# Expert loop of a mixture-of-experts block: the next round's gather and the last round's spread issued in parts between the up products

## The chip, the cores and the metric

The kernel runs on one core of a Trainium2 chip. Its engines are TensorE (PE), VectorE (DVE), ScalarE (ACT), GpSimd (POOL) and SyncE (SP), which here issues the loads. The metric is the device time of one execution in microseconds, the median of several runs; the time before is 2066.87 us.

## The reference

Two transformer blocks on 512 tokens of width 1024 in float32. The first has two kinds of attention and then a mixture of experts, which is where the change is:

```python
g_w, g_idx = lax.top_k(g_prob, 1)
top_v, top_i = lax.top_k(e_sel, TOP_K)
gate = (g_w * jax.nn.softmax(top_v, axis=-1)).reshape(-1)
def expert_block(args):
    xb, e = args
    return (jax.nn.silu(xb @ w1[e]) * (xb @ w3[e])) @ w2[e]
out = jnp.zeros((T + 1, D), jnp.float32).at[row_token].add(row_gate[:, None] * ys.astype(jnp.float32))
```

There are 64 experts; w1 and w3 are 1024 x 512 each and w2 is 512 x 1024, so one expert's weights are 6 MB and all of them 384 MB. The second block (retention and latent attention, a feed-forward layer and a gated projection) follows.

## The kernel before

The expert loop (`for q in range(NQ)`) handles four experts in each of 16 rounds, with room for 32 tokens of each, so that the four fill 128 rows or columns.

- **Loads.** A round has 24 loads of 1,024 KB: 8 pieces of w1, 8 of w3, 8 of w2 (two halves `hf` for each of four experts). `moe_load_to(n)` issues them on SyncE in that order (lines 866 and 880; 871 in the last round), into the pool `L` of 16 buffers. It is called before each half of a product with a look-ahead of `AHEAD` = 13 loads; `moe_lim` caps it until the path for overfull experts is behind. A load waits until the buffer that it takes has been read for the last time, and for the load eight before it, since SyncE counts its loads on eight semaphores in turn.
- **Up products.** `moe_up(q, k, n0)` (line 1029) multiplies the gathered tokens `xT` with w1 (k = 1) or w3 (k = 3), in two halves of 4 loads; a function handed in as `between` runs between the halves. The w1 result `p1` and the w3 result `p3` give `hd` (lines 1263 to 1265), which is transposed into `hT` (lines 1270 and 1272).
- **Gather.** `moe_gather(q)` (line 1016) picks the tokens of a round's experts by products with the 0/1 tables `oh` of `places_oh(q)` (line 998), in two halves of 32 instructions.
- **Back product.** `moe_back(q)` (line 1043) multiplies `hT` with w2 into `y`.
- **Spread.** `moe_spread(q)` transposes the gate tables `ohg` (line 1065, copied by ScalarE to `gt`), multiplies them with `y` (line 1072) and adds the result to the tokens `acc` on VectorE (line 1077), for four blocks of tokens and two halves of the width.

TensorE takes its instructions in the order of the code. In round q that is: up product 1, up product 3, both halves of the gather for round q + 1, the transposes of `hd`, the gate transposes and the whole spread of round q - 1, the back product. Every load buffer of w1 and w3 comes free at the end of a half product, those of w2 in the back product.

**The path for overfull experts.** After round 8 (`REST_AT`), `moe_rest()` loads the largest number of tokens of any expert (line 1089) into a register of each engine and, only if it is over 32, runs a body that handles what is left over (`tc.If`, line 1090). With these inputs the body isn't run. Its buffers come from the same pools as the loop's.

## Time and profile before

| what | value |
|---|---|
| median of 3 runs | 2066.87 us (2065.31 to 2069.51) |
| the profiled execution | 2066.38 us, span 2064.6 us |
| granted TensorE clock, mean of the span | 0.969 |
| TensorE busy | 1896.4 us (92% of the span) |
| VectorE, ScalarE busy | 746.8 us (36%), 468.8 us (23%) |
| moved by DMA | 510.16 MB, 247 GB/s over the span |

The profile is of one execution. A busy share is an average over stages with different limits, so the expert loop, roughly from 410 to 1365 us, is read by itself: which wait ends last there, and when SyncE may issue. Granted clock 1.00 stands for 2.4 GHz and 0.50 for 1.2 GHz.

### The profile page before, as it was taken

What the parts mean: (1) busy time and instruction counts of PE and PEld (TensorE: products, weight loads), DVE (VectorE), ACT (ScalarE), POOL (GpSimd) and SP (SyncE); (2) the same over time, 40 slices, a digit from 0 to 9 for tenths busy, and PEclk for the clock granted to TensorE, in tenths of its full rate; (3) what the DMA queues carried; (4) which work ended last, traced back from release to release, by engine and by line L of the source; (5) the groups of instructions that cost most, each with busy time, mean ns of one, the idle gap of its engine ahead of it and who ended that gap; (6) DMA issues with size and microseconds to landing.
All of it is one profiled execution on the core that took longest, in us unless ns stands there. A gap on an engine that the chain in (4) does not pass through costs nothing.

```text
span 2064.6 us, 24105 instructions
## 1 busy us (share of the span) xinstructions
PE 1896.4 (92%) x9932; PEld 1276.3 (62%) x9932; DVE 746.8 (36%) x1392; ACT 468.8 (23%) x841; POOL 208.7 (10%) x159
## 2 busy tenths in 40 slices
PE   8999999989888898887898888899999999999998
PEld 6877778744443344443344444267877788888877
DVE  4364565411111111110112310247485643434465
ACT  5454433200000000000000100044234433223232
POOL 1010001200000000000000000035034310101031
PEclk9999999999999999998999999999999999999999
DMA  8122126799999999999999999982113314141332
GB/s 278 41 73 72 42 103 210 306 393 404 407 421 417 404 407 408 404 423 386 406 417 413 419 421 419 388 284 85 41 41 113 103 41 143 48 136 54 115 133 67
DMA packets 148723, 510.16 MB, mean 247 GB/s; under 512 B 20033, under 2 KB 77178, under 8 KB 100610
## 3 DMA queue, kind: packets, MB, share of 16 engines
q1 hardware_dynamic: 144226, 501.92, 62.7%
q0 software_dynamic: 1824, 6.31, 0.8%
q8 instruction: 80, 1.31, 0.3%
q10 hardware_dynamic: 2560, 0.35, 0.1%
q14 instruction: 33, 0.27, 0.0%
HBM read 502.24 MB, written 6.31 MB: 246 GB/s over the span
## 4 chain that ended last, share of the span: by engine, by line
PE 33%; DMA 8%; issue 5%; DVE 4%; ACT 2%; POOL 1%; SPq 1%; ACTq 0%; POOLq 0%; DVEq 0%
DMA w<-in_w_dram 8%; PE g L1016 4%; PE spread L1072 3%; PE ps L1029 2%; PE g L282 2%; PE g L283 1%; PE g L284 1%; PE u L282 1%; PE u L283 1%; PE u L284 1%; PE y L1043 1%; PE d L282 1%; PE d L284 1%; PE d L283 1%; PE pg L283 1%
## 5 line engine op out<-in xcount | busy, mean ns | idle before, releaser
L1029 PE MATMUL ps<-w,xT 128*32 128x512 f32 x2040 | 345.6, 693 | 119.8 <-DMA w<-in_w_dram 113.2
L1029 PEld LDWEIGHTS ps<-w,xT 128*32 128x32 f32 x2040 | 80.7, 124 | 380.6 <-DMA w<-in_w_dram 202.4
L1016 PEld LDWEIGHTS g<-oh,x1n 128*128 128x128 f32 x1024 | 245.1, 335 | 14.3 <-issue 12.6
L1016 PE MATMUL g<-oh,x1n 128*128 128x128 f32 x1024 | 248.3, 403 | 0.8 <-DVE oh L998 0.8
L1272 ACT ACTIVATE hT<-hT 128x512 f32<-128x512 f32 x16 | 9.6, 597 | 537.6 <-PE hT L1270 537.6
L1072 PE MATMUL spread<-y,gt 128*128 128x512 f32 x256 | 114.4, 599 | 12.8 <-ACT gt L1067 12.1
L1077 DVE TENSOR_TENSOR acc<-acc,spread 128x512 f32<-128x512 f32 x128 | 88.1, 688 | 85.2 <-PE spread L1072 85.2
L1265 DVE TENSOR_TENSOR hd<-sl,ps 128x512 f32<-128x512 f32 x16 | 11.0, 687 | 278.3 <-PE ps L1029 278.3
L1043 PE MATMUL y<-w,hT 128*32 128x512 f32 x960 | 106.1, 594 | 0.7 <-ACT hT L1272 0.7
L1017 DVE TENSOR_TENSOR xT<-g,gr 128x512 f32<-128x512 f32 x32 | 22.1, 692 | 225.1 <-PE g L1016 225.1
L226 POOL TENSOR_TENSOR c0l<-c0r,c0h 128x1024 fp32r<-128x1024 f32 x2 | 4.7, 2364 | 953.1 <-ACT c0h L225 953.1
L1072 PEld LDWEIGHTS spread<-y,gt 128*128 128x128 f32 x256 | 47.2, 190 | 70.2 <-issue 38.5
L1264 DVE SCALAR_TENSOR_TENSOR sl<-sl,ps 128x512 f32<-128x512 f32 x16 | 11.0, 687 | 190.6 <-ACT sl L1263 190.6
L1043 PEld LDWEIGHTS y<-w,hT 128*32 128x32 f32 x960 | 29.7, 110 | 74.3 <-issue 66.2
L1047 ACT COPY y<-y 128x512 f32<-128x512 f32 x30 | 17.6, 586 | 199.1 <-PE y L1043 199.1
L1694 POOL TENSOR_TENSOR aTl<-sg,aTh 128x512 fp32r<-128x512 f32 x18 | 23.4, 1298 | 225.9 <-ACT aTh L1693 178.5
L1692 DVE TENSOR_TENSOR sg<-sg,u 128x512 f32<-128x512 f32 x22 | 15.1, 688 | 71.7 <-PE u L284 70.6
L1693 ACT CAST aTh<-sg 128x512 fp32r<-128x512 f32 x22 | 13.7, 621 | 104.6 <-DVE sg L1692 104.6
L1263 ACT ACTIVATE sl<-ps 128x512 f32<-128x512 f32 x16 | 9.6, 598 | 114.7 <-PE ps L1029 114.6
L174 POOL TENSOR_TENSOR rs<-ms,mhalf 128x1 f32<-128x1 f32 x20 | 12.0, 601 | 168.8 <-DVE ms L172 168.8
L1690 ACT ACTIVATE sg<-zg 128x512 f32<-128x512 f32 x22 | 13.9, 632 | 62.5 <-DVE zg L1689 62.5
L604 ACT ACTIVATE sc<-sc,mn 128x128 f32<-128x128 f32 (+3 forms) x32 | 17.7, 555 | 44.7 <-DVE mn L600 44.7
(1206 smaller groups left out, 3919.2 us busy)
## 6 DMA issues: line engine op xcount, KB each, us to landing
w<-in_w_dram SPq DMA_DIRECT2D x375, 1024.0 KB, 19.8
w<-in_w_dram SPq DMA_DIRECT2D x16, 512.0 KB, 9.6
x<-in_x_dram SPq DMA_DIRECT2D x4, 512.0 KB, 3.7
cb<-cum_d POOLq DMA_DIRECT2D x8, 256.0 KB, 3.6
acc<-in_x_dram SPq DMA_DIRECT2D x4, 512.0 KB, 7.3
e_d<-er POOLq DMA_DIRECT2D x4, 512.0 KB, 3.9
h_d<-u POOLq DMA_DIRECT2D x4, 512.0 KB, 8.0
h<-h_d SPq DMA_DIRECT2D x4, 512.0 KB, 5.4
```

The lines of the kernel that those rows point to most:

```text
L282: PE.matmul(out, ah, bh, start=(start and c == 0), stop=False)
L283: PE.matmul(out, ah, bl, start=False, stop=False)
L284: PE.matmul(out, al, bh, start=False, stop=(stop and c == kt - 1))
L604: ACT.activation(sc, sc, AF.Exp, bias=mn[:, s:s + 1], scale=-1.0, accum_out=su[:, s:s + 1])
L1016: PE.matmul(p[:, c], x1c(t)[:, 4 * hf + c], OHG[q][0][:, t].rearrange("p e s -> p (e s)"), start=(t == 0), stop=(t == NT - 1))
L1017: DVE.tensor_tensor(xT[:, 4 * hf:4 * hf + 4], p, gr[:, 4 * hf:4 * hf + 4, None].to_broadcast([128, 4, 128]), op=ALU.mult)
L1029: PE.matmul(p[32 * e:32 * e + 32], XT[q][:, 4 * hf + c, 32 * e:32 * e + 32], w[c] if isinstance(w, list) else w[:, c], start=(hf + c == 0) ...
L1043: PE.matmul(ps[nh][32 * e:32 * e + 32], HT[q][:, j, 32 * e:32 * e + 32], moe_w[2, q, hf, e][:, j - 2 * hf, 512 * nh:512 * nh + 512], start ...
L1047: ACT.copy(y[:, 512 * nh:512 * nh + 512], ps[nh])
L1072: PE.matmul(p, gt[:, t], Y[q][:, 512 * nh:512 * nh + 512], start=True, stop=True)
L1077: DVE.tensor_add(av(t)[:, sl], av(t)[:, sl], p)
L1694: (eng or POOL).tensor_sub(aT.lo(c), s_, aT.hi(c).bitcast(F32))
```

## The change

In round q the gather for round q + 1 is handed to the up products as their `between`: its first half stands between the halves of the first product, its second half between the halves of the second. The spread of round q - 1 is cut by blocks of tokens: the first two blocks follow the first up product, the other two follow the second, ahead of the transposes of `hd`. The gate transposes (`spread_gates`) are done in round q, ahead of the back product, and kept in `GT`. The place tables of round q + 2 are built after the back product of round q. In round 0 the first half of the gather stands between the halves of the second up product and the other half behind it. In the body for overfull experts the tokens are handled in two halves, with one buffer of the pool `L` in place of four and four of the pool `M` in place of two; `moe_lim` becomes 24 x 8 + 37.

```diff
--- before.py
+++ after.py
@@ -851,7 +851,7 @@
     w2p = a["w2"][0].rearrange("e (p j) n -> e p j n", j=4)
     NQ = 16
     moe_specs = [(k, q, hf, e) for q in range(NQ) for k in (1, 3, 2) for hf in range(2) for e in range(4)]
-    moe_w, moe_also, moe_n, moe_lim = {}, {}, [0], [24 * REST_AT + 34]
+    moe_w, moe_also, moe_n, moe_lim = {}, {}, [0], [24 * REST_AT + 37]
 
     def moe_load_to(n):
         n = min(n, moe_lim[0])
@@ -1076,12 +1076,13 @@
         sl = slice(512 * nh, 512 * nh + 512)
         DVE.tensor_add(av(t)[:, sl], av(t)[:, sl], p)
 
-    def moe_spread(q):
-
-        gt = spread_gates(q)
-        for t in range(NT):
+    GT = {}
+
+    def moe_spread(q, ts):
+
+        for t in ts:
             for nh in range(2):
-                spread_add(t, nh, spread_mm(q, gt, t, nh))
+                spread_add(t, nh, spread_mm(q, GT[q], t, nh))
 
     def moe_rest():
 
@@ -1090,38 +1091,42 @@
         with tc.If(most > CAP):
             gov = Sx("gov", (128, NT, 64))
             DVE.scalar_tensor_tensor(gov, rk, CAP - NOT_SEL - 0.5, gate, op0=ALU.is_ge, op1=ALU.mult)
-            hT_, hid, w2_, wk = [L("hTo"), L("hTo")], L("hido"), L("w2o"), [M("wko"), M("wko")]
+            hT_, hid, w2_, wk = L("hTo", (128, 8, 256)), M("hido", (128, 4, 256)), M("w2o"), [M("wko"), M("wko")]
+            w2q = w2_.rearrange("p (j n) -> p j n", j=4)
             ps, s_, g1 = [PS() for _ in range(4)], Sx("so"), sm("g1", (128, NT))
-            for t in range(NT):
-                for hf in range(2):
-                    p = ps[2 * (t % 2) + hf].rearrange("p (c s) -> p c s", c=4)
-                    for c in range(4):
-                        PE.transpose(p[:, c], x1c(t)[:, 4 * hf + c], ident)
-                    DVE.tensor_tensor(hT_[hf][:, :, 128 * t:128 * t + 128], p,
-                                      gr[:, 4 * hf:4 * hf + 4, None].to_broadcast([128, 4, 128]), op=ALU.mult)
-            with tc.For_i(0, 64, 1) as i:
-                DVE.tensor_scalar(g1, gov[:, :, bass.ds(i, 1)].rearrange("p t o -> p (t o)"), 0.5, None, op0=ALU.mult)
-                for f in range(4):
-                    for k, wv in enumerate((w1v, w3v)):
-                        w_ = wk[k].rearrange("p (c f) -> p c f", c=8)
-                        SP.dma_start(w_, wv[bass.ds(i, 1)].rearrange("o p c f -> (o p) c f")
-                                     [:, :, 128 * f:128 * f + 128])
-                        p = ps[2 * (f % 2) + k]
-                        for c in range(8):
-                            PE.matmul(p, w_[:, c], hT_[c // 4][:, c % 4], start=(c == 0), stop=(c == 7))
-                    ACT.activation(s_, ps[2 * (f % 2)], AF.Tanh, scale=0.5)
-                    DVE.scalar_tensor_tensor(s_, s_, 1.0, ps[2 * (f % 2)], op0=ALU.add, op1=ALU.mult)
-                    DVE.tensor_mul(hid[:, f], s_, ps[2 * (f % 2) + 1])
-                for nh in range(2):
-                    SP.dma_start(w2_, w2v[bass.ds(i, 1)].rearrange("o p j n -> (o p) j n")
-                                 [:, :, 512 * nh:512 * nh + 512])
-                    for t in range(NT):
-                        p = ps[t]
-                        for f in range(4):
-                            PE.matmul(p, hid[:, f, 128 * t:128 * t + 128], w2_[:, f], start=(f == 0), stop=(f == 3))
-                        sl = slice(512 * nh, 512 * nh + 512)
-                        DVE.scalar_tensor_tensor(av(t)[:, sl], p, g1[:, t:t + 1], av(t)[:, sl],
-                                                 op0=ALU.mult, op1=ALU.add)
+            for ts in HALVES:
+                for u, t in enumerate(ts):
+                    for hf in range(2):
+                        p = ps[2 * u + hf].rearrange("p (c s) -> p c s", c=4)
+                        for c in range(4):
+                            PE.transpose(p[:, c], x1c(t)[:, 4 * hf + c], ident)
+                        DVE.tensor_tensor(hT_[:, 4 * hf:4 * hf + 4, 128 * u:128 * u + 128], p,
+                                          gr[:, 4 * hf:4 * hf + 4, None].to_broadcast([128, 4, 128]), op=ALU.mult)
+                with tc.For_i(0, 64, 1) as i:
+                    DVE.tensor_scalar(g1, gov[:, :, bass.ds(i, 1)].rearrange("p t o -> p (t o)"), 0.5, None,
+                                      op0=ALU.mult)
+                    for f in range(4):
+                        for k, wv in enumerate((w1v, w3v)):
+                            w_ = wk[k].rearrange("p (c f) -> p c f", c=8)
+                            SP.dma_start(w_, wv[bass.ds(i, 1)].rearrange("o p c f -> (o p) c f")
+                                         [:, :, 128 * f:128 * f + 128])
+                            p = ps[2 * (f % 2) + k][:, 0:256]
+                            for c in range(8):
+                                PE.matmul(p, w_[:, c], hT_[:, c], start=(c == 0), stop=(c == 7))
+                        pg, pu = ps[2 * (f % 2)][:, 0:256], ps[2 * (f % 2) + 1][:, 0:256]
+                        ACT.activation(s_[:, 0:256], pg, AF.Tanh, scale=0.5)
+                        DVE.scalar_tensor_tensor(s_[:, 0:256], s_[:, 0:256], 1.0, pg, op0=ALU.add, op1=ALU.mult)
+                        DVE.tensor_mul(hid[:, f], s_[:, 0:256], pu)
+                    for n4 in range(4):
+                        sl = slice(256 * n4, 256 * n4 + 256)
+                        SP.dma_start(w2q, w2v[bass.ds(i, 1)].rearrange("o p j n -> (o p) j n")[:, :, sl])
+                        for u, t in enumerate(ts):
+                            p = ps[2 * (n4 % 2) + u][:, 0:256]
+                            for f in range(4):
+                                PE.matmul(p, hid[:, f, 128 * u:128 * u + 128], w2q[:, f], start=(f == 0),
+                                          stop=(f == 3))
+                            DVE.scalar_tensor_tensor(av(t)[:, sl], p, g1[:, t:t + 1], av(t)[:, sl],
+                                                     op0=ALU.mult, op1=ALU.add)
 
     AHEAD = 13
     places_oh(0)
@@ -1251,31 +1256,36 @@
         n0 = 24 * q
         if q == 12:
             cs_r, sn_r, cs_m, sn_m = rope_tables()
+
+        nxt = [] if q + 1 == NQ else [lambda hf=hf: moe_gather(q + 1, (hf,)) for hf in range(2)]
         if q:
-            p1 = moe_up(q, 1, n0)
-        if q + 1 < NQ:
-            places_oh(q + 1)
-            places_gate(q + 1)
+            p1 = moe_up(q, 1, n0, nxt.pop(0) if nxt else None)
+            moe_spread(q - 1, HALVES[0])
         else:
-            moe_spread(q - 1)
-        p3 = moe_up(q, 3, n0 + 8)
+            places_oh(1)
+            places_gate(1)
+        p3 = moe_up(q, 3, n0 + 8, nxt.pop(0) if nxt else None)
         sl_, hd = Sx("sl"), Sx("hd")
         ACT.activation(sl_, p1, AF.Tanh, scale=0.5)
         DVE.scalar_tensor_tensor(sl_, sl_, 1.0, p1, op0=ALU.add, op1=ALU.mult)
         DVE.tensor_mul(hd, sl_, p3)
-        if q + 1 < NQ:
-            moe_gather(q + 1)
+        if q:
+            moe_spread(q - 1, HALVES[1])
+        for go in nxt:
+            go()
         ph = PS("hT", (128, 4, 128))
         for j in range(4):
             PE.transpose(ph[:, j], hd.rearrange("s (p j) -> s j p", j=4)[:, j], ident)
         HT[q] = Sx("hT", (128, 4, 128))
         ACT.mul(HT[q], ph, 0.5)
-        if 0 < q < NQ - 1:
-            moe_spread(q - 1)
         if q + 1 < NQ:
+            GT[q] = spread_gates(q)
             moe_back(q, n0 + 16)
         else:
             moe_back_half(q, n0 + 16, 0)
+        if q + 2 < NQ:
+            places_oh(q + 2)
+            places_gate(q + 2)
         if q == REST_AT:
             moe_rest()
             moe_lim[0] = len(moe_specs)
```

The order of TensorE's instructions from one up product to the back product shows the move. `ps` is the up product, `g` the gather, `rk` the gate transposes; the first instruction of each piece stands for it. Before, in round 5:

```order
L1029 MATMUL ps_4672<-w_883_4521,xT_4544 32x512
...
L1029 MATMUL ps_4731<-w_911_4652,xT_4544 32x512
...
L1016 MATMUL g_4786<-oh_4721,x1n_3070 128x128
...
L1016 MATMUL g_4804<-oh_4721,x1n_3070 128x128
...
L1270 MATMUL hT_4822<-cst,hd_4781 128x128 x4
L1065 MATMUL rk_4829<-cst,ohg_4244 128x128 x4
L1072 MATMUL spread_4836<-y_4619,gt_4834 128x512
...
L1043 MATMUL y_4861<-w_920_4703,hT_4827 32x512
```

The change, the same round:

```order
L1029 MATMUL ps_4689<-w_892_4577,xT_4473 32x512
...
L1016 MATMUL g_4715<-oh_4679,x1n_3070 128x128
...
L1029 MATMUL ps_4689<-w_909_4635,xT_4473 32x512
...
L1072 MATMUL spread_4757<-y_4626,gt_4624 128x512
...
L1029 MATMUL ps_4769<-w_913_4659,xT_4473 32x512
...
L1016 MATMUL g_4794<-oh_4679,x1n_3070 128x128
...
L1029 MATMUL ps_4769<-w_920_4696,xT_4473 32x512
...
L1072 MATMUL spread_4841<-y_4626,gt_4624 128x512
...
L1278 MATMUL hT_4853<-cst,hd_4837 128x128 x4
L1065 MATMUL rk_4860<-cst,ohg_4443 128x128 x4
L1043 MATMUL y_4868<-w_926_4739,hT_4858 32x512
```

The two halves of the gather and of the spread have moved from behind both up products to places in and after each of them, and the gate transposes now stand ahead of the back product with no spread behind them.

The second place is SyncE's queue ahead of the branch after round 8 (`w13` and `w2` are the weight pieces, `cmax_i` the largest count). Before:

```order
L866 DMA w2_1074_5483<-in_w2_dram 128x2048
L880 DMA w13_1075_5485<-in_w1_dram 128x2048
...
L880 DMA w13_1103_5616<-in_w3_dram 128x2048
L1089 TENSOR_LOAD cmax_i_3540
...
L1090 COMPARE_AND_BRANCH
```

The change:

```order
L866 DMA w2_1083_5539<-in_w2_dram 128x2048
L880 DMA w13_1084_5541<-in_w1_dram 128x2048
...
L880 DMA w13_1105_5623<-in_w3_dram 128x2048
L1090 TENSOR_LOAD cmax_i_3540
...
L1091 COMPARE_AND_BRANCH
```

In both, eight loads of w1 and one of w3 of round 9 stand between the last load of w2 of round 8 and the branch; nothing moved here.

## Rows read from the trace of the kernel before

**Rows 1.** The page's 40 slices of 51.6 us: DMA busy in tenths, GB/s.

```profile
DMA  8122126799999999999999999982113314141332
GB/s 278 41 73 72 42 103 210 306 393 404 407 421 417 404 407 408 404 423 386 406 417 413 419 421 419 388 284 85 41 41 113 103 41 143 48 136 54 115 133 67
```

**Rows 2.** The page's DMA issues: count, KB each, median us to landing.

```profile
w<-in_w_dram SPq DMA_DIRECT2D x375, 1024.0 KB, 19.8
```

**Rows 3.** SyncE's waits, 430 to 1320 us: total us, times, longest.

```profile
SPq L880 <- PE y L1043: 241.0, 30, 15.9
SPq L880 <- DMA w<-in_w_dram: 235.2, 123, 2.5
...
SPq L1090 <- SPq L1090: 8.9, 1, 8.9
```

**Rows 4.** Chain of waits, round 10: start, us, what.

```profile
1027.88 3.62 PE ps L1029 x26
1031.50 15.43 PE g L1016 x64
...
1048.57 7.13 PE spread L1072 x16
1055.70 3.69 PE y L1043 x32
...
1067.63 19.82 DMA w<-in_w_dram
```

**Rows 5.** By stretch: busy us of each engine, then PE clock, DMA share, GB/s.

```profile
502.00:508.00 6.00, 6.00 (x60) 1.82 (x56) 0.91 (x5) 0.87 (x2) 0.00 (x0) 1.00 0.77 277
...
941.00:949.00 8.00, 7.52 (x56) 2.23 (x60) 0.00 (x0) 0.00 (x0) 0.00 (x0) 0.73 0.58 214
...
1128.00:1134.00 6.00, 3.38 (x28) 0.81 (x20) 2.13 (x5) 0.00 (x0) 0.00 (x0) 1.00 0.93 363
1301.00:1307.00 6.00, 6.00 (x60) 1.82 (x56) 0.00 (x0) 1.17 (x2) 0.00 (x0) 1.00 0.79 283
```

**Rows 6.** The same view: three longer stretches.

```profile
1140.00:1300.00 160.00, 138.79 (x718) 74.06 (x714) 33.90 (x68) 10.12 (x17) 0.00 (x0) 0.95 1.01 420
430.00:940.00 510.00, 435.46 (x2338) 219.41 (x2338) 81.74 (x170) 24.51 (x43) 0.00 (x0) 0.94 1.00 411
950.00:1320.00 370.00, 318.26 (x1700) 159.00 (x1692) 69.91 (x134) 23.42 (x38) 0.00 (x0) 0.94 1.00 415
```

**Rows 7.** TensorE's timeline: start, us, line, tile, count [idle before].

```profile
397.36 3.64 PE L1029 MATMUL ps<-w,xT 128*32 128x512 f32 x32 [0.83 <-issue]
...
716.81 5.22 PE L1029 MATMUL ps<-w,xT 128*32 128x512 f32 x26 [1.44 <-DMA w<-in_w_dram]
...
746.23 7.07 PE L1043 MATMUL y<-w,hT 128*32 128x512 f32 x64
```

**Rows 8.** The page's groups: line, tile, count, busy us, mean ns, idle before.

```profile
L1272 ACT ACTIVATE hT<-hT 128x512 f32<-128x512 f32 x16 | 9.6, 597 | 537.6 <-PE hT L1270 537.6
...
L1265 DVE TENSOR_TENSOR hd<-sl,ps 128x512 f32<-128x512 f32 x16 | 11.0, 687 | 278.3 <-PE ps L1029 278.3
```

**Rows 9.** TensorE's timeline, last round, as rows 7.

```profile
1331.59 5.04 PE L1029 MATMUL ps<-w,xT 128*32 128x512 f32 x26 [1.55 <-DMA w<-in_w_dram]
...
1338.84 2.40 PE L1058 MATMUL y<-w,hT 128*32 128x256 f32 x36 [0.69 <-ACT hT L1272]
...
1343.58 1.91 PE L1058 MATMUL y<-w,hT 128*32 128x256 f32 x26 [0.83 <-DMA w<-in_w_dram]
```

**Rows 10.** Line 1090, the branch: count, ns min/median/max, first and last start.

```profile
L1090 SPq EVENT_SEMAPHORE  x8: 17/17/17, 944.1 to 944.7; - x8
...
L1090 PEldq COMPARE_BRANCH  x1: 6832/6832/6832, 934.3 to 934.3; - x1
```

**Rows 11.** By stretch, as rows 5: the granted clock within one run of products.

```profile
716.81:720.10 3.29, 3.29 (x16) 0.79 (x20) 0.00 (x0) 0.00 (x0) 0.00 (x0) 0.50 1.01 418
720.10:721.90 1.80, 1.80 (x14) 0.34 (x6) 0.00 (x0) 0.00 (x0) 0.00 (x0) 1.00 1.04 423
```

## The prediction

> **What bounds the kernel now.** I read the page's slices first, then the list of transfers, SyncE's waits, the chain of waits, and the rate of the DMA engines by stretch. In the slices the middle of the span, nearly half of it, is a stretch with the DMA engines at 9 tenths and about 400 GB/s or a little over [rows 1]. That is the expert loop, which reads 24 loads of 1,024 KB of weights in each of 16 rounds. The reader is to see that the rate is high but not flat. One 1 MB load takes 19.8 us from its issue to its landing [rows 2]. At 420 GB/s that is 8.3 MB, so about eight loads are under way at once and one lands every 2.5 us. SyncE's waits say why the rate is not flat [rows 3]. Its 123 waits for earlier loads, 235 us, are harmless: the queue is full then. Its 30 waits for the back products (y), 241 us and up to 15.9 us each, are not: SyncE has no free buffer and issues nothing.
>
> The chain of waits shows the circle for one round [rows 4]. TensorE ends the second up product, runs the whole gather of the next round (15.43 us), the transposes, the spread of the round before (7.13 us) and the first half of the back product (3.69 us), and only then does a buffer come free; the loads go out, and the next queue of them takes 19.82 us to land. From 1031.50, the end of the up product, to 1059.39, the end of that half, TensorE frees no buffer for 27.9 us. The queue covers 19.8 us of that, and what was free before the burst covers most of the rest. What is left is a hole of DMA time: of the 6 us windows at the ends of the bursts, eight look like the first and the last of [rows 5], at 277 and 283 GB/s; the other rounds have a shallower one or none. So loads bound this loop, TensorE sets when they can start, and TensorE's own work is not the bound.
>
> **The sum of the holes.** In a stretch with hardly a hole the engines move 420 GB/s (1140 to 1300). Over 430 to 940 us they moved 411, over 950 to 1320 us 415 [rows 6]. At 420 the same bytes would have taken 510 x 9/420 = 10.9 us and 370 x 5/420 = 4.4 us less: 15.3 us. Checked from the other side: a window at 277 GB/s has lost 6 x (1 - 277/420) = 2.0 us, and eight of them 16 us.
>
> **Gather and spread in parts.** Nothing is added: the same 64 gather, 16 spread and 8 transpose instructions a round run on TensorE, in other places. The longest stretch without a freed buffer becomes half a gather and half an up product. Half a gather is 15.43/2 = 7.7 us; half an up product is 3.64 us at full clock, and 5.22 us for 26 of its 32 instructions where it began at the half clock [rows 7]. So 11.4 to about 13 us in place of 27.9, under the 19.8 us that the queue covers. The other stretch is half a spread (3.6 us), the transposes with their copies (1.6 us, the gap between gather and spread in [rows 4]) and half a back product (7.07/2 = 3.5 us), 8.7 us. TensorE must also keep up: four half products (14.6), the gather (15.4), the spread (7.1), the back product (7.1) and those 1.6 us are 45.8 us a round. A round of 24 loads of 1.049 MB takes 59.9 us at 420. So 14 us of slack are left. I expect every hole of [rows 5] that belongs to a burst to go. What is late next is DMA itself. The window at 1128 us stays: it is the round with the loads of the rotary positions, at 363 GB/s, and costs 0.8 us. Gain: 15.3 - 0.8 = 14.5 us by the stretches, 16 by the windows; I take 15, with 12 and 17 as ends, since the holes may have hidden small delays that will now show.
>
> **What is queued behind the moved steps.** The second half of the spread now stands between the last up product and the transposes of hd. VectorE forms hd in 0.7 us [rows 8] meanwhile, so this is cover and not a wait, and the gather that covered it before is not missed. After the transposes ScalarE's copy hT is no longer covered by the spread but by the transposes of the gates alone, so TensorE may stand for up to the copy's 0.6 us [rows 8]; the 14 us of slack take that. The place tables are built a round earlier, behind the back product, so the gather finds them ready. SyncE's order of loads is the same, and no POOL work is moved. In the last round there is no such slack. There the last up product runs to about 1336.6 and y begins at 1338.84, waits for its loads, and ends at 1345.5 [rows 9]. With 3.6 us of spread in between, which covers the 0.7 us of hd, y begins 2.9 us later, at 1341.7, and its 64 instructions need 64 x 1.91/26 = 4.7 us: 1346.4, some 0.8 us later than now. That is a cost of 0.8 us, at least nothing and at most the 3.6 us of the half spread.
>
> **The path for overfull experts.** It isn't taken: at L1090 each engine loads the largest count and branches past the body. Its price now is one window of 8 us at 214 GB/s [rows 5], 8 x (1 - 214/420) = 3.9 us. SyncE's own rows say where it is from. Behind the branch it stands 8.9 us [rows 3] and then takes its eight semaphore steps of 17 ns from 944.1 to 944.7 [rows 10], one for each of its load counters; I read that as a wait until all loads under way have landed. The raised limit (37 in place of 34) would let three more loads go ahead of the branch, but in the order of SyncE's instructions the same load, the first of w3 in round 9, is still the last one before it: the look-ahead of 13 ends there first (8 x 24 + 20 + 13 = 225 loads, under both limits, 226 and 229). And loads ahead of a drain only move the drain. So I cost this edit at nothing: the 3.9 us stay. Bounds: a gain of 3.9 us if I misread the wait, and a loss of 6.8 us, the branch on TensorE [rows 10], if the larger body made SyncE fetch code for as long behind an empty queue.
>
> **Sum.** The profiled execution took 2066.38 us; its span is 2064.6 and 1.8 us lie around it. 2066.38 - 15 + 0.8 = 2052.2. That execution is 0.5 us under the median of the runs, so for the median I say 2052.5 us. What follows the loop, from about 1346 us, waits for the last loads and moves forward as a whole.
>
> **Rivals.** (a) *The clock makes TensorE the bound: slower.* TensorE runs at half speed behind each wait: the granted clock was 0.50 from 716.81 to 720.10 and 1.00 from there on, inside one unbroken run of products [rows 11]. Now the long burst that ran at full speed is cut into pieces between waits. If all the work behind a wait stayed at half speed, the products, gather and spread would take 2 x (14.6 + 15.4 + 7.1) = 74.2, with 8.7 for the rest 82.9 us a round, 23 more than the loads, over 15 rounds 344 us: about 2410 us. It decides once more than 14/45.8, 31%, of the work runs at half speed. Against it: if each of the four half products starts cold, the extra is 5.22 - 26 x 3.64/32 = 2.3 us each, 9 us a round, inside the 14; and an engine that falls behind has no waits left, and [rows 11] show the clock back within one run. The Trainium skill, "TensorE: Matmul & The Clock Gate", section "HAM oscillation — how this bites in real kernels", speaks against this change in the same sense: groups of matmuls shorter than the waits for their data start throttled every time. By that rule taken alone the time would be rival (a)'s; the trace agrees that the clock falls in the waits (0.50) and shows that it returns inside one half product.
>
> (b) *The hole only moves: no gain.* If the lag of TensorE at the half gathers ran the queue dry as the burst does now, the time would stay at about 2067. For it: the holes come from the same two steps. Against: this needs 19.8 us without a freed buffer, and the longest stretch is 13.
>
> (c) *Half a gain.* The holes go, but delays that they hid (a load of which one piece comes late) show in every round, or the last round takes its full 3.6 us: 2067 - 7 = 2060 at the middle of 2057 to 2062.
>
> (d) *The branch gets cheaper too.* The 3.9 us go as well: 2052.5 - 3.9 = 2048.6. Against it stands the unchanged place of the last load; so for the raised limit the change would not do what it says, and the forecast has it so.
>
> **How the numbers follow.** Forecast 72%, with 2050 to 2056 as its own range (gains of 17 and 12, the last round between nothing and 1.6 us); (a) 3%, (b) 7%, (c) 10%, (d) 8%. A measurement of this kernel tells 0.2%, 4.1 us, from no change. Faster by more than that are the forecast, (d) and (c): 0.90. Same is (b), 0.07; slower is (a), 0.03. The range takes in the forecast, (d) with the upper gain (2046.5) and (c) to its middle: 2046.5 to 2060. Left out are (a), (b) and half of (c), 15%.
>
> **What would show it.** In the profile after: SyncE's waits for y fall from 241 us to almost nothing and its waits for earlier loads grow; the windows at the round's ends read about 420; gather rows stand in halves of 7.7 us between the products; the rounds repeat every 59.6 to 60 us; the eight steps behind the branch still come after some 20 us, with a hole of 3.5 to 4.5 us. Wrong it would be if SyncE waits for the up products in turn with holes there, if TensorE's waits for loads vanish while the round is longer than 61 us (a), or if the loop ends 15 us sooner and the part behind it takes longer.

## The result and the profile after

| | before | changed kernel |
|---|---|---|
| median of the runs | 2068.19 us (4 runs, 2065.31 to 2069.92) | 2052.05 us (4 runs, 2050.07 to 2054.89) |
| profiled execution | 2066.38 us | 2050.91 us |
| its span | 2064.6 us | 2048.8 us |
| mean granted clock | 0.969 | 0.974 |

The ratio is 0.9924, with a 95% interval of 0.9906 to 0.9943: faster by 0.76%, about 16 us. The forecast was 2052.5 us. From profile to profile the span lost 15.8 us.

First the page's slices of the changed kernel (DMA busy in tenths, GB/s), which answer to [rows 1]:

```profile
DMA  8122125799999999998999999973113214141342
GB/s 280 37 78 70 45 103 212 285 397 422 421 421 420 421 421 421 421 421 370 421 421 420 421 421 421 395 246 100 27 52 117 90 42 144 52 134 57 114 133 67
```

In [rows 1] the middle went up and down between 386 and 423 GB/s. Now it is flat at 420 to 422, with one slice at 370. The rate by stretch says the same in finer grain (columns as in [rows 5]; the last is GB/s):

```profile
430.00:940.00 510.00, 452.19 (x2443) 227.54 (x2445) 83.31 (x173) 25.58 (x45) 0.00 (x0) 0.96 1.00 415
950.00:1320.00 370.00, 323.29 (x1677) 152.36 (x1677) 66.74 (x131) 22.33 (x36) 0.00 (x0) 0.93 1.01 420
430.00:920.00 490.00, 433.55 (x2343) 216.50 (x2343) 80.56 (x169) 24.99 (x44) 0.00 (x0) 0.96 1.01 421
960.00:1300.00 340.00, 296.97 (x1555) 140.24 (x1544) 62.10 (x124) 21.73 (x35) 0.00 (x0) 0.93 1.01 421
926.00:938.00 12.00, 12.00 (x65) 8.40 (x65) 1.24 (x2) 0.60 (x1) 0.00 (x0) 1.00 0.53 200
```

The loop ends sooner now, so the first two lines take in other work than in [rows 6]. The next two are the loop ahead of the branch and behind it without its edges: 421 GB/s in both, so no hole at the end of a round is left. The last line is the one hole that is left, at the branch past the body for overfull experts: 12 x (1 - 200/421) = 6.3 us of DMA time.

SyncE's waits from 430 to 1320 us (us in total, times, longest), against [rows 3]:

```profile
SPq L880 <- DMA w<-in_w_dram: 460.2, 219, 3.6
...
SPq L1091 <- SPq L1091: 18.5, 1, 18.5
SPq L880 <- PE y L1043: 15.6, 12, 11.4
```

The wait for a back product fell from 241.0 to 15.6 us. The wait at line 880 for earlier loads, which is the harmless one (the queue is full), grew from 235.2 to 460.2 us. The wait behind the branch grew from 8.9 to 18.5 us.

TensorE's timeline of round 6 (start, us, line, tile, count, idle time before) shows the new order:

```profile
740.93 3.62 PE L1029 MATMUL ps<-w,xT 128*32 128x512 f32 x26 [1.45 <-DMA w<-in_w_dram]
744.48 7.88 PE L1016 MATMUL g<-oh,x1n 128*128 128x128 f32 x32
752.29 3.64 PE L1029 MATMUL ps<-w,xT 128*32 128x512 f32 x32
755.86 3.70 PE L1072 MATMUL spread<-y,gt 128*128 128x512 f32 x8
...
760.82 3.62 PE L1029 MATMUL ps<-w,xT 128*32 128x512 f32 x26 [0.27 <-DMA w<-in_w_dram]
764.37 7.89 PE L1016 MATMUL g<-oh,x1n 128*128 128x128 f32 x32
772.19 3.64 PE L1029 MATMUL ps<-w,xT 128*32 128x512 f32 x32
775.76 3.70 PE L1072 MATMUL spread<-y,gt 128*128 128x512 f32 x8
779.30 0.63 PE L1278 MATMUL hT<-cst,hd 128*128 128x128 f32 x4
779.77 0.60 PE L1065 MATMUL rk<-cst,ohg 128*128 128x128 f32 x4
780.68 4.48 PE L1043 MATMUL y<-w,hT 128*32 128x512 f32 x34 [0.31 <-ACT hT L1280]
```

Half a gather stands between two half products, half a spread behind each product. From the end of one half product to the end of the next (744.55 to 755.93, 764.44 to 775.83) there are 11.4 us. In [rows 4] TensorE freed no buffer for 27.9 us.

### The profile page after: what moved, and what is told of

It is laid out like the page before. It is cut to its first block, busy times and chain, and to the rows that moved or that the text cites. A ratio compares the mean times of both kernels' runs of the same rounds, so it can differ in the third digit from the quotient of the medians.

```text
span 2048.8 us, 24118 instructions
## 1 busy us (share of the span) xinstructions
PE 1905.1 (93%) x9932; PEld 1274.1 (62%) x9932; DVE 744.6 (36%) x1392; ACT 468.4 (23%) x841; POOL 208.8 (10%) x159
## 4 chain that ended last, share of the span: by engine, by line
PE 25%; DMA 18%; issue 5%; DVE 4%; ACT 1%; POOL 1%; SPq 0%; ACTq 0%; POOLq 0%; DVEq 0%
DMA w<-in_w_dram 18%; PE g L282 2%; PE g L284 2%; PE g L283 2%; PE u L282 1%; PE u L284 1%; PE u L283 1%; PE d L282 1%; PE d L284 1%; PE d L283 1%; PE pg L283 1%; PE pg L284 1%; PE pg L282 1%; PE ps L1029 1%; DVE h L1639 1%
## 5 line engine op out<-in xcount | busy, mean ns | idle before, releaser
L1029 PE MATMUL ps<-w,xT 128*32 128x512 f32 x2040 | 301.2, 627 | 60.2 <-DMA w<-in_w_dram 55.3
L1029 PEld LDWEIGHTS ps<-w,xT 128*32 128x32 f32 x2040 | 71.4, 114 | 255.5 <-issue 128.6
L1043 PE MATMUL y<-w,hT 128*32 128x512 f32 x960 | 171.5, 686 | 48.3 <-DMA w<-in_w_dram 43.6
L1043 PEld LDWEIGHTS y<-w,hT 128*32 128x32 f32 x960 | 39.5, 122 | 166.6 <-DMA w<-in_w_dram 84.9
L1703 ACT CAST aTh<-sg 128x512 fp32r<-128x512 f32 x22 | 13.7, 621 | 105.0 <-DVE sg L1702 105.0
L768 POOL TENSOR_TENSOR mTl<-gl,mTh 128x512 fp32r<-128x512 f32 x8 | 11.5, 1454 | 157.7 <-PE ps L284 145.8
## 6 DMA issues: line engine op xcount, KB each, us to landing
w<-in_w_dram SPq DMA_DIRECT2D x375, 1024.0 KB, 19.8
```

The lines of the kernel that those rows point to most:

```text
L1029: PE.matmul(p[32 * e:32 * e + 32], XT[q][:, 4 * hf + c, 32 * e:32 * e + 32], w[c] if isinstance(w, list) else w[:, c], start=(hf + c == 0) ...
L1043: PE.matmul(ps[nh][32 * e:32 * e + 32], HT[q][:, j, 32 * e:32 * e + 32], moe_w[2, q, hf, e][:, j - 2 * hf, 512 * nh:512 * nh + 512], start ...
```

## The experiments

The theory: the loop is bound by loads; before, the burst of gather and spread left TensorE without freeing a buffer for longer than the queue and the free buffers cover, and what stood out was a hole. Cutting the stretch below the cover removes the hole, and no more is to be had there. The rivals: the gain comes from one of the two moves alone, from other places of the loads, from the new body for overfull experts, or TensorE is close behind as the next bound.

### One part alone: the gather, then the spread

The kernel before, with the gather alone in halves between the halves of the up products; the spread whole in its old place:

```diff
+        nxt = [] if q + 1 == NQ else [lambda hf=hf: moe_gather(q + 1, (hf,)) for hf in range(2)]
         if q:
-            p1 = moe_up(q, 1, n0)
...
+            p1 = moe_up(q, 1, n0, nxt.pop(0) if nxt else None)
...
-        p3 = moe_up(q, 3, n0 + 8)
+        p3 = moe_up(q, 3, n0 + 8, nxt.pop(0) if nxt else None)
```

> The kernel before with the gather alone moved between the halves of the up products; the spread stays whole, behind the transposes of hd. Theory (a hole opens when TensorE frees no buffer for more than about 26 us; 27.9 us before): the longest stretch is then 1.6 + 7.1 + 3.7 = 12.4 us, so every hole goes and the time is that of the whole change, about 2052 us (2049 to 2055). Rival (gather and spread each carry their share, by length 15.4 to 7.1): two thirds of the gain, about 2057 us. No effect without the spread: 2067 us.

Measured: 2052.37 us (6 runs, 2049.88 to 2054.50) against 2067.78 before, ratio 0.9919, interval 0.9901 to 0.9936. Its stretch ahead of the branch (the one behind it, 960 to 1300 us, reads 421 as well) and its waits of SyncE:

```profile
430.00:920.00 490.00, 427.91 (x2339) 218.79 (x2338) 80.58 (x169) 24.50 (x43) 0.00 (x0) 0.96 1.01 421
```

```profile
SPq L880 <- PE y L1043: 41.8, 24, 11.4
SPq L1090 <- SPq L1090: 18.4, 1, 18.4
```

The whole gain, and every hole at the end of a round gone. The hole at the branch is left.

Now the changed kernel with the gather put back behind both products, so that the spread alone is in parts:

```diff
-            p1 = moe_up(q, 1, n0, nxt.pop(0) if nxt else None)
+            p1 = moe_up(q, 1, n0)
...
-        p3 = moe_up(q, 3, n0 + 8, nxt.pop(0) if nxt else None)
+        p3 = moe_up(q, 3, n0 + 8)
```

> The change with the gather put back whole behind the up products; the spread stays in two parts. Theory: the stretch without a freed buffer falls from 27.9 to 27.9 - 3.6 = 24.3 us, just under the 26 us at which a hole opens, so nearly all of the gain stays: about 2053 us (2050 to 2057). Rival (gain by the length of what is moved): one third, 2062 us, or a sixth for half a spread, 2065 us.

Measured: 2049.57 us (6 runs, 2049.03 to 2053.26), ratio 0.9911, interval 0.9893 to 0.9929. The same two views (421 behind the branch too):

```profile
430.00:920.00 490.00, 429.21 (x2313) 217.36 (x2317) 80.58 (x169) 23.83 (x42) 0.00 (x0) 0.95 1.01 421
```

```profile
SPq L880 <- PE y L1043: 193.5, 30, 13.5
SPq L1091 <- SPq L1091: 10.9, 1, 10.9
```

The whole gain again. The gains of the two parts don't add up: each alone is enough. The second fence is the one to remember. SyncE still waits for the back products 30 times, 193.5 us in all, nearly as long as before (241.0), and no DMA time is lost by it. By the sum, taking half the spread (3.6 us) out of the burst brings the 27.9 us down to 24.3. In round 5 of this run the last up product ends at 715.1 us and the first half of the back product at 738.6, 23.5 us later: TensorE's wait of 0.8 us for the gate tables has gone too. So the hole opens somewhere between 23.5 and 27.9 us, and a wait of SyncE of up to 13.5 us is still covered by the loads that are under way.

### Two edits that change nothing

The kernel before with a longer look-ahead:

```diff
-    AHEAD = 13
+    AHEAD = 16
```

> The kernel before with a look-ahead of 16 loads in place of 13, nothing moved. Theory (the holes are a lack of loads sent ahead): up to three loads more, 2.5 us each, go out before the burst, so the 2 us holes close with no step moved: about 2053 us. Rival (what counts is the order on TensorE): no change, 2067 us, with SyncE's waits for y still some 240 us and the holes at 280 GB/s.

Measured: 2068.92 us (12 runs, 2062.89 to 2080.12), ratio 1.0005, interval 0.9987 to 1.0022. This is a miss of the experiment's design: no more loads went ahead. SyncE's waits for y hardly moved, 239.1 us in 31 waits. The constant only moves the place in the program where a load is written down. Which buffer it takes, and so whose reader it waits for, follows from the number of buffers, and that was the same. The next pair of runs changes that number.

The kernel before with the new body and the limit of 37 alone:

```diff
-    moe_w, moe_also, moe_n, moe_lim = {}, {}, [0], [24 * REST_AT + 34]
+    moe_w, moe_also, moe_n, moe_lim = {}, {}, [0], [24 * REST_AT + 37]
...
-            hT_, hid, w2_, wk = [L("hTo"), L("hTo")], L("hido"), L("w2o"), [M("wko"), M("wko")]
+            hT_, hid, w2_, wk = L("hTo", (128, 8, 256)), M("hido", (128, 4, 256)), M("w2o"), [M("wko"), M("wko")]
```

> The kernel before with the new body for overfull experts and the raised limit alone. Theory: the last load before the branch is the same, and the drain behind it is the same hole of 3.9 us: no change, 2067 us within 2 us. Rival (the three more loads fill the hole): 2063 us. Rival (the larger body costs a longer branch): up to 2074 us.

Measured: 2067.28 us (12 runs, 2058.51 to 2074.15), ratio 0.9995, interval 0.9979 to 1.0010. SyncE stood 9.3 us behind the branch, before 8.9. Alone, the new body changes nothing that can be seen, and the gain is not from it.

### One buffer less, in both kernels

```diff
-NL, NM, NS = 16, 11, 13
+NL, NM, NS = 15, 11, 13
```

In the kernel before:

> The kernel before with 15 load buffers in the pool L in place of 16. Theory: each buffer is one load of 2.5 us that can be sent ahead of the burst, so every round's hole grows by 2.5 us: 14 rounds, +35 us, about 2102 us (2092 to 2112; the pool is used outside the loop as well), with holes of 4 to 5 us. Rival (the holes come from the order on TensorE, not from buffers): under 2072 us.

Measured: 2110.12 us (4 runs, 2106.73 to 2112.32), ratio 1.0196, interval 1.0166 to 1.0225: 41.5 us slower. One window at the end of a round, and the long stretch:

```profile
503.00:511.00 8.00, 8.00 (x73) 2.37 (x76) 2.54 (x10) 1.07 (x2) 0.00 (x0) 1.00 0.46 162
...
430.00:940.00 510.00, 427.22 (x2241) 211.54 (x2240) 73.80 (x153) 22.25 (x39) 0.00 (x0) 0.94 0.96 397
```

A window of 8 us at 162 GB/s has lost 8 x (1 - 162/421) = 4.9 us, and such windows stand at the ends of other rounds too (156 GB/s from 824 us, 166 from 1340 us). One buffer is one load of about 2.5 us; gather and spread stand together in the 14 rounds from 1 to 14, and 41.5 us over 14 bursts is 3.0 us for each. The whole loss lies there: added up in windows of 2 us, the ends of these bursts lost some 59 us in this profile and some 18 in that of the kernel before.

In the changed kernel, the same edit:

> The changed kernel with 15 load buffers. Theory: the longest stretch without a freed buffer is about 13 us, so one load less ahead opens no hole and the loop stays at 421 GB/s: 2052 us, up to 2057 with what the smaller pool costs outside the loop. Rival (the change only made the hole as small as the cover, or the gain came from elsewhere): +35 us as before, 2087 us.

Measured: 2052.75 us (4 runs, 2051.77 to 2053.78), ratio 0.9923 to the kernel before, interval 0.9895 to 0.9951. Both stretches read 421 GB/s. The buffer that was worth 41.5 us before is worth nothing that can be seen now. This pair, with the two runs of one part alone, is what shows the theory: the price is the part of the stretch that stands out over what the buffers cover.

### How far off is TensorE?

The changed kernel with the first half of the gather done twice, from the gather for round 2 on, which runs in round 1; that is 7.8 us more a round (`TWICE = (0,)`), and then with both halves (`TWICE = (0, 1)`), 15.6 us more:

```diff
         for hf in hfs:
             p = PS("g", (128, 4, 128))
-            for c in range(4):
-                for t in range(NT):
-                    PE.matmul(p[:, c], x1c(t)[:, 4 * hf + c], ...)
+            for _ in range(2 if hf in TWICE and q > 1 else 1):
+                for c in range(4):
+                    for t in range(NT):
+                        PE.matmul(p[:, c], x1c(t)[:, 4 * hf + c], ...)
```

> The changed kernel with the 32 instructions of the gather's first half run twice from round 1 on (7.8 us more on TensorE a round, the result is the same). Theory (14 us of slack on TensorE): 45.8 + 7.8 = 53.6 us a round, under the 59.9 of the loads, and the stretch without a freed buffer becomes some 21 us, under 26: no hole, 2052 us (to 2056). Rival (the clock has eaten the slack, 9 us a round in cold starts): TensorE becomes the bound, 45.8 + 9 + 7.8 = 62.6 us a round, +2.7 in 14 rounds, 2090 us.

Measured: 2052.13 us (4 runs, 2048.55 to 2053.48), ratio 0.9921, interval 0.9893 to 0.9948, 420 and 421 GB/s in the two stretches. TensorE does 7.8 us more work a round, and the time stays the same.

> The changed kernel with both halves of the gather run twice from round 1 on (15.6 us more on TensorE a round). Theory (14 us of slack, and an engine without waits keeps the full clock): 45.8 + 15.6 = 61.4 us a round and some 0.3 us behind the copy hT, against 59.7 of the loads: TensorE is the bound by 2 us in 14 rounds, +28 us, about 2080 us (2072 to 2090). Rival (cold starts of 9 us a round stay): 70.4 us a round, +150 us, 2200 us. Rival (more slack than counted): 2052 us.

Measured: 2061.46 us (8 runs, 2059.69 to 2064.22), ratio 0.9956, interval 0.9941 to 0.9971. That is 9.4 us over the changed kernel, which was timed in another set of runs, and below the expected range of 2072 to 2090 us. Its stretch ahead of the branch, and TensorE's timeline of one round:

```profile
430.00:920.00 490.00, 487.64 (x2777) 328.55 (x2778) 78.14 (x160) 22.76 (x40) 0.00 (x0) 1.00 1.01 415
```

```profile
679.25 7.07 PE L1045 MATMUL y<-w,hT 128*32 128x512 f32 x64 [0.31 <-ACT hT L1282]
686.14 3.62 PE L1031 MATMUL ps<-w,xT 128*32 128x512 f32 x32
689.69 15.48 PE L1018 MATMUL g<-oh,x1n 128*128 128x128 f32 x64
...
739.81 5.78 PE L1045 MATMUL y<-w,hT 128*32 128x512 f32 x51 [0.31 <-ACT hT L1282]
```

Now TensorE is the bound: busy 487.64 of 490 us, with no pause for loads between the pieces, the clock at 1.00 throughout, and 415 GB/s. A round takes 739.81 - 679.25 = 60.56 us. Without the 15.6 that were added TensorE's own work is 45.0 us a round. In the changed kernel the transposes of `hd` come at 481.05 us in round 1 and at 898.58 in round 8, seven rounds of 59.65 us in the mean. The slack is 14.6 us. The expectation had 45.8 us of work and so 61.7 us a round; 60.56 - 59.65 is 0.9 us a round, 13 us in 14 rounds.

### The branch past the body

The changed kernel, with the loads of the body, which is not run here, issued by POOL in place of SyncE:

```diff
-                            SP.dma_start(w_, wv[bass.ds(i, 1)].rearrange("o p c f -> (o p) c f")
+                            POOL.dma_start(w_, wv[bass.ds(i, 1)].rearrange("o p c f -> (o p) c f")
...
-                        SP.dma_start(w2q, w2v[bass.ds(i, 1)].rearrange("o p j n -> (o p) j n")[:, :, sl])
+                        POOL.dma_start(w2q, w2v[bass.ds(i, 1)].rearrange("o p j n -> (o p) j n")[:, :, sl])
```

> The changed kernel with the loads inside the body for overfull experts issued by GpSimd in place of SyncE (the body isn't run). Theory (SyncE's stand of 18.5 us behind the branch is a wait until its loads under way have landed, set by the body's use of the same load counters): SyncE goes past the branch in under 1 us, the hole of 6.1 us goes, 2046 us (2044 to 2049). Rival (the stand is the fetch of code behind a taken branch): SyncE still stands 6 us or more, the queue covers up to 19.8 us of it, and there may be no hole either, but the rows will show the stand. Rival (no gain): 2052 us.

Measured: 2046.58 us (6 runs, 2045.85 to 2048.47), ratio 0.9893 to the kernel before, interval 0.9871 to 0.9914. This is the fastest kernel here: 22 us under the kernel before, and by the medians 5.5 us under the changed kernel, which was timed in another set of runs; the two intervals overlap a little. In its own set the changed kernel with 15 buffers, which reads 421 GB/s in the same stretches, took 2051.77 us at the least, more than any run of this one. First the rows of line 1091 in the changed kernel (count, ns min/median/max, first and last start), then the same rows here, then its rate across that place:

```profile
L1091 SPq EVENT_SEMAPHORE  x8: 17/17/17, 933.7 to 934.2; - x8
...
L1091 PEldq COMPARE_BRANCH  x1: 5946/5946/5946, 912.1 to 912.1; - x1
L1091 SPq COMPARE_BRANCH  x1: 50/50/50, 915.2 to 915.2; - x1
```

```profile
L1091 POOLq EVENT_SEMAPHORE  x4: 17/43/43, 413.8 to 414.0; - x4
...
L1091 PEldq COMPARE_BRANCH  x1: 6006/6006/6006, 911.0 to 911.0; - x1
L1091 SPq COMPARE_BRANCH  x1: 50/50/50, 914.0 to 914.0; - x1
```

```profile
920.00:960.00 40.00, 39.78 (x206) 23.58 (x207) 7.72 (x12) 0.60 (x1) 0.00 (x0) 0.96 1.01 421
```

In the changed kernel SyncE's branch takes 50 ns at 915.2, and its eight semaphore steps come at 933.7: in between it stands until its loads have landed. Here SyncE has no such steps; POOL has four of its own at 413.8, long before. The next load goes out about 1.2 us behind the branch, and the rate has no dent. TensorE's branch is as long as before. Taking its loads out also makes SyncE's body shorter, so this run alone does not rule out that the stand was a fetch of code. The other runs do: with the same new body SyncE stands 9.3 us in the kernel before, 10.9 with the spread alone moved and 18.5 in the changed kernel, and 18.4 with the old body and the gather alone moved; and in the changed kernel the steps come when the rate has just reached 0 (49 GB/s in the microsecond from 932, 0 in the next). The stand follows the queue and not the body. It is the wait for SyncE's own queue, and that wait is there because the body behind the branch issues loads on that queue.

The same edit in the kernel before:

> The kernel before with the loads inside the body for overfull experts issued by GpSimd. Theory: the stand of 8.9 us and the hole of 3.9 us behind the branch go, the holes of the rounds stay: 2064 us (2062 to 2066). Rival (the hole behind the branch hides one of the burst's holes, which now opens): 2066 us or no change.

Measured: 2066.79 us (12 runs, 2060.18 to 2071.36), ratio 0.9987, interval 0.9971 to 1.0003: nothing that can be told from no change. A gain of the expected size, 3.9 us or a ratio of 0.998, lies inside the interval as well. In the profile the hole at the branch is gone, and two rounds have holes that the profile of before has not (first this kernel, then the windows of before that answer to the last two):

```profile
941.00:949.00 8.00, 8.00 (x52) 2.24 (x51) 0.00 (x0) 0.00 (x0) 0.00 (x0) 0.67 1.01 423
...
1178.00:1184.00 6.00, 6.00 (x64) 1.81 (x60) 1.02 (x6) 0.76 (x2) 0.00 (x0) 1.00 0.68 239
1240.00:1246.00 6.00, 6.00 (x64) 1.81 (x60) 1.00 (x5) 0.78 (x2) 0.00 (x0) 1.00 0.74 261
```

```profile
1179.00:1185.00 6.00, 6.00 (x60) 1.82 (x56) 0.40 (x2) 1.17 (x2) 0.00 (x0) 1.00 1.00 395
1240.00:1246.00 6.00, 6.00 (x63) 1.82 (x56) 0.00 (x0) 1.17 (x2) 0.00 (x0) 1.00 0.99 399
```

The two windows of this kernel lost 6 x (2 - (239 + 261)/421) = 4.9 us, those of before 6 x (2 - (395 + 399)/421) = 0.7. So in this one profile the 3.9 us of the branch came back in other rounds. That the edit does this is not shown: the kernel before with the new body alone keeps its hole at the branch (221 GB/s from 941 to 949 us), and its profile has deep holes in late rounds too (284 GB/s from 1122 to 1128, 246 from 1185 to 1191). Which rounds have them differs between profiles as long as the bursts stand. The edit is worth 5.5 us where the holes are closed; where they are open, 12 runs that scatter over 11 us can't tell 3.9 us from nothing.

## Why the prediction was right, point by point

**The sum of the holes: right, a little too small.** Predicted 15.3 us by the stretches. With 421 GB/s, which the changed kernel holds, [rows 6] give 510 x 10/421 = 12.1 and 370 x 6/421 = 5.3, together 17.4 us. A rounding of half a GB/s in these rows is about 1 us, so the two values hardly differ.

**Gather and spread in parts: right.** The expected 11.4 us between freed buffers are there to the tenth (round 6 above), all holes at the ends of rounds are gone, SyncE's waits have turned over from y to earlier loads, and the rounds ahead of the branch repeat every 59.65 us (expected 59.6 to 60). What the working did not see is how little was needed: it argued that the stretch must come under the 19.8 us that the queue covers. Spread alone leaves 23.5 us and has no hole. The free buffers ahead of the burst, which the text named and then left out, cover at least 3.7 us more. It also took SyncE's waits for y as the harm itself; with the spread alone moved 193.5 of their 241 us are still there, and no hole.

**The window at 1128 us: wrong, and small.** It was to stay, at 0.8 us, as a cost of the loads of the rotary positions. In the kernel before this load was issued at 1120.8 us, behind a wait for the back product of 13.7 us. It is now issued at 1099.8 us, lands 18.0 us later, and the windows of 6 us from 1108 to 1126 read 415 to 424 GB/s. The hole went with the burst; by what steps it came 8 us behind the burst's end no run shows.

**TensorE's slack: right.** Counted as 45.8 us a round, with 14 us to spare. The run with both halves of the gather twice gives 45.0 and 14.6. ScalarE's copy hT, which the spread no longer covers, makes TensorE stand 0.31 us a round (round 6 above); 0.6 was the bound, and the slack takes it.

**The last round: a term of 0.8 us that was not there.** Its end in the changed kernel, against [rows 9]:

```profile
1315.86 5.37 PE L1029 MATMUL ps<-w,xT 128*32 128x512 f32 x26 [0.66 <-DMA w<-in_w_dram]
1321.16 3.70 PE L1072 MATMUL spread<-y,gt 128*128 128x512 f32 x8
1324.70 0.63 PE L1278 MATMUL hT<-cst,hd 128*128 128x128 f32 x4
1326.02 3.72 PE L1058 MATMUL y<-w,hT 128*32 128x256 f32 x64 [0.69 <-ACT hT L1280]
```

From the end of the last up product to the end of y there were 1345.49 - 1336.63 = 8.9 us, and now there are 1329.74 - 1321.23 = 8.5. The added half of the spread fills the time in which y had waited for its loads, and behind it y runs through without a stop, 58 ns an instruction and 3.72 us in all. I had priced 4.7 us from the 26 instructions at the end of [rows 9], which are 73 ns each. The y of the last round ends 15.75 us sooner, and so does the span: what follows the loop did not get longer.

**The branch: mis-sized, by 2.4 us.** I read the wait rightly (the run with the body's loads on POOL shows it), and the raised limit did nothing, as the order had shown. But I kept the cost at 3.9 us, with 3.5 to 4.5 as what would be seen; it is 6.3. With a full queue at the branch the stand is 18.5 us in place of 8.9; that it would be some 20 was foreseen, that the hole grows with it was not. The run with the gather alone has a stand of 18.4 us and 12 x (1 - 195/421) = 6.4 us lost there. How the queue empties has changed too; the last section has the rows.

**Round 0: a difference that I did not see.** In the window from 409 to 415 us the up product of round 0 ran partly at the half clock before (first line); now it has the full one (second line):

```profile
409.00:415.00 6.00, 5.39 (x36) 1.40 (x40) 5.26 (x25) 0.44 (x3) 0.00 (x0) 0.72 0.59 250
```

```profile
409.00:415.00 6.00, 5.33 (x52) 1.72 (x56) 5.26 (x25) 1.03 (x3) 0.00 (x0) 1.00 0.77 283
```

The product frees its buffers sooner, and over 400 to 430 us the rate is 351 GB/s in place of 330: 30 x 21/421 = 1.5 us. All profiles with gather or spread moved have the full clock there as well. But so has the kernel before with the body's loads on POOL, whose order in round 0 is the old one, with 351 GB/s over 400 to 430 us; two others of the old order, with the longer look-ahead and with one buffer less, read 0.72 as before. So the old order does not always bring the half clock, and that these 1.5 us are a gain of the change is not shown.

**The sum.** 17.4 from the stretches, less 2.4 at the branch, nothing at the last round: 15.0 us, or 16.5 with the 1.5 of round 0, where the span lost 15.8. My own terms were 15 less 0.8, 14.2. So the prediction is right for its main reason; of its errors, holes too small by 2.4 us and a branch too cheap by 2.4 cancelled, and 0.8 at the last round was too dear. That the median came within 0.5 us of the forecast is luck in part: the forecast was 14.4 us below 2066.87, the median of 3 runs of the kernel before, and against 2068.19, the median of 4, the gain is 16.1.

**The rivals.** (a) *The clock* did what the rival says in one place: the starts at the half clock moved. The page's groups of the up and the back product, first before, then after (busy us, mean ns | idle before):

```profile
L1029 PE MATMUL ps<-w,xT 128*32 128x512 f32 x2040 | 345.6, 693 | 119.8 <-DMA w<-in_w_dram 113.2
...
L1043 PE MATMUL y<-w,hT 128*32 128x512 f32 x960 | 106.1, 594 | 0.7 <-ACT hT L1272 0.7
```

```profile
L1029 PE MATMUL ps<-w,xT 128*32 128x512 f32 x2040 | 301.2, 627 | 60.2 <-DMA w<-in_w_dram 55.3
...
L1043 PE MATMUL y<-w,hT 128*32 128x512 f32 x960 | 171.5, 686 | 48.3 <-DMA w<-in_w_dram 43.6
```

The back product, which ran in one piece behind the burst, now waits for loads between its instructions and has become slower in the mean, 594 to 686 ns; the up products have become faster, 693 to 627 ns. The slack pays for it. And the rival has no hold: the run in which TensorE is the bound has next to no waits left ahead of the branch (0.31 us a round) and the clock at 1.00. The prediction's words, half speed behind each wait, say too much: in round 6 above the 26 instructions from 740.93 us, behind a wait of 1.45, take 3.62 us, and their granted clock was 1.00. In the back product of the same round the groups of two between the waits ran at 1.00 (785 to 790 us), and 0.50 came in the longer group of 25 behind them (791 to 793). The Trainium skill, "TensorE: Matmul & The Clock Gate", "HAM oscillation — how this bites in real kernels", has a group of matmuls that is shorter than the wait for its data start throttled, every time. The trace agrees with it in part: clock is lost behind such waits, but not at every start, and here the waits are slack. (b) *The hole only moves* fell: SyncE waits for the up products 23 times for 7.4 us at line 880, with no hole at the end of a round. (c) *Half a gain* fell with the stretches at 421 GB/s. (d) *A cheaper branch* did not come with the change; it took another edit.

## What to carry to other kernels

In a loop bound by loads, look for the longest stretch in which no buffer is freed, and compare it with what is queued plus what is free: only what stands out over that costs time, so a cut below it gets the whole gain and further cuts get none. A long wait of the loading engine is no evidence of a loss in itself (193.5 us of it cost nothing here); read the rate of the DMA engines beside it. A body that is branched past still costs when it issues loads on the busy queue, because the queue is emptied first (6.3 us of DMA time here); issue them from another one, and expect to see the gain only where no larger holes scatter the time.

## What the runs showed that was not expected

**A queue that was never empty drains out of step.** In the kernel before, the rate at the branch fell from full to 25 GB/s in two microseconds. In the changed kernel it takes six. Single microseconds there:

```profile
926.00:927.00 1.00, 1.00 (x6) 1.00 (x5) 0.00 (x0) 0.00 (x0) 0.00 (x0) 1.00 1.04 434
928.00:929.00 1.00, 1.00 (x6) 1.00 (x6) 0.00 (x0) 0.00 (x0) 0.00 (x0) 1.00 0.61 254
930.00:931.00 1.00, 1.00 (x6) 1.00 (x5) 0.00 (x0) 0.00 (x0) 0.00 (x0) 1.00 0.39 164
932.00:933.00 1.00, 1.00 (x8) 0.75 (x11) 0.17 (x1) 0.00 (x0) 0.00 (x0) 1.00 0.17 49
```

The busy share goes 1.04, 0.61, 0.39, 0.17: some of the 16 engines are done while others still have work. I take it that the holes of the kernel before brought the engines back into step once a round; that is argued, not shown. The other runs fit: the fall takes two to three microseconds with the new body alone and with one buffer less in the kernel before, and four to six with gather alone and spread alone.

**TensorE's branch is dear, SyncE's is not.** The same branch took 5946 ns on TensorE and 50 ns on SyncE. TensorE's product behind it waited 3.3 us, which the slack took. The Trainium skill, "Runtime: NRT & Kernel Launch", "Instruction fetch mechanics", has a taken branch to code that is not loaded wait for its fetch. TensorE's row would fit that, and no run here tells it from another cause, or why the rows of the other engines are short.
